# A state-space stage whose convolution of x moves from channels on partitions to tokens on partitions

## The chip, the cores and the metric

The kernel runs on one core of one Trainium2 chip. The core has TensorE (PE, matrix products into PSUM), VectorE (DVE, elementwise), ScalarE (ACT, functions and copies), GpSimd (POOL, elementwise on SBUF) and SyncE (SP, which only issues transfers), each with its own queue of instructions in the order in which the program wrote them, and 16 DMA engines that all queues share. The metric is the device time of one execution in microseconds, the median of several runs.

## The reference

The model is a decoder trunk of two layers on 256 tokens with 2048 features: a latent attention, a dense squared-ReLU MLP, a Mamba-2 state-space mixer and a second MLP, each behind an RMS norm and added to a residual stream. All of it is float32. The change is in the state-space mixer:

```python
def ssm_mixer(h, w_in, conv_w, conv_b, dt_bias, a_log, d_skip, norm_g, w_out):
    zxbcdt = h @ w_in                       # 256 x 2048 by 2048 x 10304
    z, xbc, dt = jnp.split(zxbcdt, [4096, 4096 + 6144], axis=-1)
    xbc = silu(causal_depthwise_conv(xbc, conv_w, conv_b))   # 4 taps over tokens, per channel
    xs, b_in, c_in = jnp.split(xbc, [4096, 4096 + 1024], axis=-1)
    dt = softplus(dt + dt_bias)
    a = -exp(a_log)
    y = ssd_chunked_scan(xs, dt, a, b_in, c_in)   # 8 groups of 8 heads of 64 features
    y = y + d_skip * xs
    y = y * silu(z)
    y = y * rsqrt(mean(y * y, per group) + eps) * norm_g
    return y @ w_out
```

The convolution gives each channel at token s the sum of its own four weights times that channel at tokens s-3 to s, plus a bias. The scan is one chunk of 256 tokens: per head a 256 x 256 matrix of decays times scores, applied to x times dt.

## The kernel before

Every weight matrix is streamed from HBM in units of 128 x 1024 float32 (512 KB): SP issues the load into one of six `raw` buffers (line 88), ACT copies it to a rounded half `wh` (line 103), DVE subtracts to get the remainder `wl` (line 104), and TensorE forms three products per tile, high by high, high by low and low by high (`products`, lines 362 to 364). `Flow.next` keeps loads up to six units and conversions three units ahead of TensorE; there are four `wh` and four `wl` buffers, so ACT's copy for a unit waits until TensorE has left the unit four before it. A unit in the state-space stage is twelve products of 512 columns.

`ssm_body` holds the stage. Its token list is `SSM_ORDER` (line 1441): blocks of eight units for B, C, x and z (512 output columns each, both halves of the tokens t = 0, 1 in two PSUM banks of 128 tokens x 512 channels), the narrow block for dt, and pieces of the output product (`o`, four units for each of four column blocks) as soon as two groups are gated. TensorE's order is written out by this list; what the other engines do, and TensorE's small products, is put between units by a small planner: `when(us, fn)` puts a function into a list with a due time, `small` does the same and keeps small TensorE work 2.6 apart, and `move(2.72)` after each unit advances the planner's clock and calls what has come due. A function called there writes its instructions at that place of every engine's queue.

One x block is one group of eight heads. After its last unit `x_done` evacuates the two banks (`evac`, line 1117), and `conv` works in two halves of 256 channels: four 128 x 128 transposes bring channels onto partitions (line 1128), ACT starts the sum with bias and fourth weight (line 1135), DVE adds the three shifted terms, a shift being an offset in the free dimension (line 1138, three per 128 channels), ACT takes the Silu (line 1139). Then `back(t)` transposes four times per half of the tokens (line 1257), copies out (line 1260), multiplies by dt on DVE (line 1262) and by the decay to the chunk's edge and by d on POOL (lines 1266, 1271), and queues the group in `waiting`. `heads(g)`, one group at a time, loads four decay rows spread to 128 partitions (`cm`, SP, line 1298), forms exponents and decays on ACT (lines 1305, 1309), multiplies by the scores `cb` on DVE (line 1313), and `product` applies them to x on TensorE (line 1322). `gate` multiplies by Silu of z, normalizes, and transposes for the output product (`turn`, line 1368). B and C go through the same `conv`.

The only waits that bind the queues to each other here are those on buffers: `scratch` tiles (eight), `xtm` (six) and `xd` (four) for x and x times dt, four `cm`, four PSUM banks for small work and four for accumulation.

Of the kernel before, what the change touches and what calls it, by code (L numbers as in the profile page):

```python
# [20 lines left out]
F32 = mybir.dt.float32  # L21
F32R = mybir.dt.float32r
I32 = mybir.dt.int32
AF = mybir.ActivationFunctionType
ALU = mybir.AluOpType
# [3 lines left out]
P = 128  # L29
# [7 lines left out]
GROUPS = 8  # L37
# [177 lines left out]
class Banks:  # L215
    name = "bank"
# [14 lines left out]
class Trunk:  # L231
# [849 lines left out]
    def ssm_body(self, sp, dp, gain):  # L1081
        nc, d, cst = self.nc, self.d, self.cst
        lhs_x = self.from_tiles(self.xT)
        xT, rs = self.xT, self.rs
# [13 lines left out]
        def small(us, fn, gap=2.6):  # L1098
            at[1] = max(at[0] + us, at[1] + gap)
            when(at[1] - at[0], fn)  # L1100
# [10 lines left out]
        diagonal = lambda: cst[:, C_TRI:C_TRI + P]  # L1111

        def evac(accs):
            ev = []
            for t in range(2):
                e = self.scratch()
                nc.scalar.activation(e, accs[t], AF.Copy, scale=rs[t])
                ev.append(e)
            return ev
# [38 lines left out]
        def cb_group(g):  # L1158
# [5 lines left out]
            t = sp.tile([P, 2, P], F32, name=f"cb{g}")  # L1164
            far[g] = sp.tile([P, 2, P], F32R, name=f"cf{g}")
# [77 lines left out]

        def x_done(g, accs):
            fmx = [None, None]
            ev = evac(accs)
            xg[g], xd[g] = [None, None], [None, None]

            def dst(j, a):
                fmx[j] = a  # L1250
                return a

            def back(t):
                b = self.ps(self.sm, "sm")
                for k in range(4):
                    o = (k % 2) * 256 + t * P
                    nc.tensor.transpose(b[:, k * P:(k + 1) * P], fmx[k // 2][:, o:o + P], self.ident)
                at[0] += 0.45
                x = sp.tile([P, 512], F32, tag="xtm", name=f"xtm{g}_{t}", bufs=XTM)
                nc.scalar.activation(x, b, AF.Copy)  # L1260
                w = sp.tile([P, 512], F32, tag="xd", name=f"xd{g}_{t}", bufs=XD)
                nc.vector.tensor_tensor(heads_of(w), heads_of(x), spread(dt[:, t], g), ALU.mult)
                xg[g][t], xd[g][t] = x, w
                if t == 0:
                    xw = self.scratch()
                    nc.gpsimd.tensor_tensor(heads_of(xw), heads_of(x), spread(edge[:, 0], g), ALU.mult)
                    xh = sp.tile([P, 512], F32R, tag="xh", name=f"xh{g}", bufs=1)
                    xl = self.s2.tile([P, 512], F32R, tag="s2", name=self.name("s2"))
                    self.split_out(xh, xl, xw)
                    small(8, lambda: across(xh, xl))  # L1270
                nc.gpsimd.tensor_tensor(heads_of(x), heads_of(x), spread(cst[:, C_DSK:C_DSK + 64], g), ALU.mult)
                if t:
                    waiting.append(g)
                    if len(waiting) == 1:
                        heads(g)
# [11 lines left out]
            def after():  # L1287
                small(10, lambda: back(0))
                small(10, lambda: back(1))

            conv(ev, 4 * g, dst, after)

        def heads(g):
# [43 lines left out]
            begin = 24 if g == 1 else 0  # L1337
# [12 lines left out]
        def gate(g):  # L1350
# [21 lines left out]
            lag = 14 if g == 1 else 10  # L1372
# [3 lines left out]

        done = {"B": lambda i, a: bc_done("B", i, a), "C": lambda i, a: bc_done("C", i, a), "x": x_done, "z": z_done}
# [44 lines left out]
XTM, XD = 6, 4  # L1422


def ssm_plan():
    out = []
    for step in SSM_ORDER:
# [7 lines left out]
        else:  # L1435
# [5 lines left out]
SSM_ORDER = ["B0", "dt0", "C0", "x0", "x1", "B1", "C1", "z0", "z1", "x2", "x3", "o0", "z2", "z3", "x4", "x5", "o1",  # L1441
             "z4", "z5", "x6", "x7", "o201", "z6", "z7", "o223"]
# [198 lines left out]
```

## Time and profile before

| what | value |
|---|---|
| median of three runs | 2307.21 us (2306.47 to 2308.12) |
| the profiled execution's own time | 2306.98 us |
| its span | 2305.2 us |
| TensorE busy | 2294.9 us |
| DVE busy | 1854.1 us |
| ACT busy | 1432.4 us |
| POOL busy | 182.7 us |
| granted TensorE clock | 1.00 throughout |

The profile is of one execution. Its page gives busy time per engine, the span in 40 slices, the DMA queues, the chain of work that ended last, the costliest groups of instructions by line, and the DMA issues with the median time from issue to landing. A group's row reads: line, engine, operation, what it writes and reads, count, total busy us, mean ns; then the engine's idle time before these instructions and what ended it. Products of TensorE overlap, so their single durations do not add up; distances between starts do. The state-space stage lies at about 969 to 1560 us.

### The profile page before, as it was taken

Reading aid. Unit: us, or ns where it says so; the run is one execution under the profiler, and the core shown is the slowest. Engines: PE = TensorE matmul, PEld = TensorE weight load, DVE = VectorE, ACT = ScalarE, POOL = GpSimd, SP = SyncE. Lnnn points to the kernel's source line nnn. Section 1 sums busy time; section 2 is a strip of 40 time slices with the busy share of each in tenths; the row PEclk is TensorE's granted clock in tenths of the full one; section 3 lists DMA queues with packets and bytes.
Section 4 is the critical chain, followed back from the end, with each engine's and each line's share of the span. In section 5 each row is a group of like instructions: output and inputs, shape, how many; then the busy total and the mean of one; then the engine's idle time right before and its main releaser. Section 6 shows DMA issues by size and latency. Waiting matters only on the chain.

```text
span 2305.2 us, 30566 instructions
## 1 busy us (share of the span) xinstructions
PE 2294.9 (100%) x11065; PEld 1905.9 (83%) x11065; DVE 1854.1 (80%) x2180; ACT 1432.4 (62%) x1986; POOL 182.7 (8%) x223
## 2 busy tenths in 40 slices
PE   9999999999999999999999999999999999999999
PEld 7888888888888888888888888888888888888887
DVE  7776697999899897677677676766989889889895
ACT  7775465566666656576656566565666656666663
POOL 1430000000000000001010111110000000000000
PEclk9999999999999999999999999999999999999999
DMA  8444687887887877655566656566687788787874
GB/s 320 146 132 151 205 233 240 265 240 247 265 244 248 267 215 241 197 184 182 187 198 193 207 177 214 187 193 201 203 260 231 251 266 249 239 270 240 250 229 161
DMA packets 146102, 508.68 MB, mean 221 GB/s; under 512 B 16480, under 2 KB 17184, under 8 KB 145952
## 3 DMA queue, kind: packets, MB, share of 16 engines
q1 hardware_dynamic: 137664, 477.30, 62.8%
q0 software_dynamic: 8064, 29.36, 7.7%
q8 instruction: 87, 1.43, 0.2%
q14 instruction: 63, 0.52, 0.1%
q10 hardware_dynamic: 224, 0.07, 0.0%
HBM read 504.51 MB, written 2.16 MB: 220 GB/s over the span
## 4 chain that ended last, share of the span: by engine, by line
PE 97%; issue 1%; DVE 1%; DMA 0%; ACT 0%; POOL 0%; SPq 0%; DVEq 0%; ACTq 0%; POOLq 0%
PE yp L363 9%; PE yp L364 9%; PE yp L362 9%; PE acc L362 8%; PE acc L364 8%; PE acc L363 8%; PE st L363 8%; PE st L364 8%; PE st L362 8%; PE acc L345 3%; PE acc L341 3%; PE acc L342 3%; PE sm L326 2%; PE a L341 1%; PE kv L341 1%
## 5 line engine op out<-in xcount | busy, mean ns | idle before, releaser
L104 DVE TENSOR_TENSOR wl<-wraw,wh 128x1024 fp32r<-128x1024 f32 (+2 forms) x818 | 991.6, 1226 | 307.3 <-ACT wh L103 298.0
L103 ACT ACTIVATE wh<-wraw 128x1024 fp32r<-128x1024 f32 (+2 forms) x818 | 858.0, 1053 | 574.8 <-PE yp L364 178.2
L363 PE MATMUL yp<-wl,k 128*128 128x512 f32 x896 | 348.9, 389 | 1.0 <-DVE wl L104 1.0
L362 PE MATMUL yp<-wh,k 128*128 128x512 f32 x896 | 349.8, 390 | 0.0
L364 PE MATMUL yp<-wh,k 128*128 128x512 f32 x896 | 348.8, 389 | 0.0
L362 PE MATMUL acc<-wh,xt 128*128 128x512 f32 x704 | 279.3, 397 | 0.0
L363 PE MATMUL acc<-wl,xt 128*128 128x512 f32 x704 | 274.4, 390 | 0.4 <-DVE wl L104 0.4
L364 PE MATMUL acc<-wh,xt 128*128 128x512 f32 x704 | 274.7, 390 | 0.0
L103 ACT ACTIVATE wh<-wrx 128x1024 fp32r<-128x1024 f32 x168 | 177.9, 1059 | 136.4 <-PE yp L364 109.5
L104 DVE TENSOR_TENSOR wl<-wrx,wh 128x1024 fp32r<-128x1024 f32 x168 | 204.0, 1220 | 36.6 <-ACT wh L103 36.3
L363 PEld LDWEIGHTS yp<-wl,k 128*128 128x128 f32 x896 | 168.3, 188 | 36.3 <-DVE wl L104 1.9
L364 PEld LDWEIGHTS yp<-wh,k 128*128 128x128 f32 x896 | 168.2, 188 | 35.0
L362 PEld LDWEIGHTS yp<-wh,k 128*128 128x128 f32 x896 | 168.3, 188 | 34.6
L362 PE MATMUL st<-wh,xt 128*128 128x512 f32 x448 | 176.8, 395 | 0.0
L363 PE MATMUL st<-wl,xt 128*128 128x512 f32 x448 | 174.8, 390 | 0.0
L364 PE MATMUL st<-wh,xt 128*128 128x512 f32 x448 | 174.8, 390 | 0.0
L364 PEld LDWEIGHTS acc<-wh,xt 128*128 128x128 f32 x704 | 132.1, 188 | 28.1
L363 PEld LDWEIGHTS acc<-wl,xt 128*128 128x128 f32 x704 | 132.4, 188 | 27.1 <-DVE wl L104 1.2
L362 PEld LDWEIGHTS acc<-wh,xt 128*128 128x128 f32 x704 | 132.3, 188 | 26.1 <-issue 0.2
L199 POOL DMA_DIRECT2D wrx<-mi x56 | 49.0, 876 | 1140.8 <-DVE wl L104 988.6
L362 PE MATMUL st<-wh,sN 128*128 128x512 f32 x336 | 132.3, 394 | 0.0
L364 PE MATMUL st<-wh,sN 128*128 128x512 f32 x336 | 130.9, 390 | 0.0
(318 smaller groups left out, 3558.4 us busy)
## 6 DMA issues: line engine op xcount, KB each, us to landing
wraw<-mi SPq DMA_DIRECT2D x256, 512.0 KB, 5.2
wraw<-mo SPq DMA_DIRECT2D x256, 512.0 KB, 5.2
wraw<-si SPq DMA_DIRECT2D x160, 512.0 KB, 4.4
wraw<-so SPq DMA_DIRECT2D x64, 512.0 KB, 4.1
wrx<-mi SPq DMA_DIRECT2D x56, 512.0 KB, 5.0
wrx<-mi POOLq DMA_DIRECT2D x56, 512.0 KB, 8.0
wraw<-wo SPq DMA_DIRECT2D x32, 512.0 KB, 3.9
wraw<-ukv SPq DMA_DIRECT2D x16, 512.0 KB, 4.5
```

Source lines behind the costliest of these rows:

```text
L103: self.last = nc.scalar.activation(h[:, v], raw[:, v], AF.Copy)
L104: nc.vector.tensor_tensor(lo[:, v], raw[:, v], h[:, v].bitcast(F32), ALU.subtract)
L199: nc.gpsimd.dma_start(st["b11"].tile, quarter(d, 1, 0), accum_op=ALU.add)
L326: self.nc.tensor.transpose(b[:, j * P:(j + 1) * P], src[:, j * P:(j + 1) * P], self.ident)
L341: nc.tensor.matmul(accs[t][:, :n], ah, wh[:, q, :], start=first and kt + q == 0, stop=False)
L342: nc.tensor.matmul(accs[t][:, :n], al, wh[:, q, :], start=False, stop=False)
L345: nc.tensor.matmul(accs[t][:, :n], lhs(kt + q, t)[0], wl[:, q, :], start=False, stop=en and q == nk - 1)
L362: nc.tensor.matmul(b, ah, wh, start=first and q == 0, stop=False)
L363: nc.tensor.matmul(b, ah, wl, start=False, stop=False)
L364: nc.tensor.matmul(b, al, wh, start=False, stop=last and q == 1)
```

## The change

x stays with tokens on partitions. After an x block ACT evacuates both banks, scaled, into one tile `ev` of 128 tokens x 2 halves of the channels x 2 halves of the tokens x 256 channels. For each half of the channels, `shifted` makes three shifted copies in `ex`: for a shift by m tokens the ACT queue issues a transfer inside SBUF of 128 - m rows of 2 KB to m partitions further down, and the GpSimd queue one of m rows of 1 KB that carries the last m tokens of the first token half to the first partitions of the second. The planner places `weighted` seven of its microseconds later, in four steps 2.2 apart on DVE: the three copies times their weights in one operation (1536 elements per partition), the unshifted one times its weight and plus the bias, two additions, the last addition, and then ACT's Silu straight into `xtm`. The weights and bias of 256 channels come spread to all partitions, from a new input `cx`, by SP, as one transfer of 640 KB per half into a single buffer, asked for after the second step of the half before. `finish` does what `back` did behind its copy. Groups go through this one at a time (`line`). x and z blocks alternate, B1 and C1 come later, the output pieces are dealt out differently, the scores have six buffers instead of eight, and group 1's later start (`begin`, `lag`) goes. B and C keep `conv`.

```diff
@@ -1109,6 +1109,9 @@
         heads_of = lambda v: v.rearrange("p (h f) -> p h f", h=8)
         spread = lambda v, g: v[:, 8 * g:8 * g + 8].unsqueeze(2).to_broadcast([P, 8, 64])
         diagonal = lambda: cst[:, C_TRI:C_TRI + P]
+        ex, ev, tap = sp.tile([P, 3, 2, 256], F32, name="ex"), sp.tile([P, 2, 2, 256], F32, name="ev"), {}
+        line = []
+        nc.gpsimd.memset(ex[0:3, :, 0], 0.0)
 
         def evac(accs):
             ev = []
@@ -1161,8 +1164,8 @@
             nc.tensor.matmul(b[:, 0:256], B[:, 0:P], C, start=True, stop=True)
             nc.tensor.matmul(b[:, 256:384], B[:, P:256], C[:, P:256], start=True, stop=True)
             at[0] += 0.65
-            t = sp.tile([P, 2, P], F32, name=f"cb{g}")
-            far[g] = sp.tile([P, 2, P], F32R, name=f"cf{g}")
+            t = sp.tile([P, 2, P], F32, tag="cb", name=f"cb{g}", bufs=6)
+            far[g] = sp.tile([P, 2, P], F32R, tag="cf", name=f"cf{g}", bufs=6)
             for i in range(2):
                 nc.vector.tensor_tensor(t[:, i], b[:, 2 * i * P:2 * i * P + P], diagonal(), ALU.mult)
             self.split_out(far[g][:, 0], far[g][:, 1], b[:, P:256])
@@ -1241,38 +1244,79 @@
 
             small(15, cums)
 
+        def taps(k):
+            if k < 2 * GROUPS:
+                w = sp.tile([P, 5, 256], F32, tag="cx", name=f"cx{k}", bufs=1)
+                nc.sync.dma_start(w.rearrange("p a n -> p (a n)"), d["cx"][k:k + 1].to_broadcast([P, 5 * 256]))
+                tap[k] = w
+
         def x_done(g, accs):
-            fmx = [None, None]
-            ev = evac(accs)
+            line.append((g, accs))
+            if len(line) == 1:
+                x_begin(g, accs)
+
+        def x_begin(g, accs):
             xg[g], xd[g] = [None, None], [None, None]
-
-            def dst(j, a):
-                fmx[j] = a
-                return a
-
-            def back(t):
-                b = self.ps(self.sm, "sm")
-                for k in range(4):
-                    o = (k % 2) * 256 + t * P
-                    nc.tensor.transpose(b[:, k * P:(k + 1) * P], fmx[k // 2][:, o:o + P], self.ident)
-                at[0] += 0.45
-                x = sp.tile([P, 512], F32, tag="xtm", name=f"xtm{g}_{t}", bufs=XTM)
-                nc.scalar.activation(x, b, AF.Copy)
-                w = sp.tile([P, 512], F32, tag="xd", name=f"xd{g}_{t}", bufs=XD)
-                nc.vector.tensor_tensor(heads_of(w), heads_of(x), spread(dt[:, t], g), ALU.mult)
-                xg[g][t], xd[g][t] = x, w
-                if t == 0:
-                    xw = self.scratch()
-                    nc.gpsimd.tensor_tensor(heads_of(xw), heads_of(x), spread(edge[:, 0], g), ALU.mult)
-                    xh = sp.tile([P, 512], F32R, tag="xh", name=f"xh{g}", bufs=1)
-                    xl = self.s2.tile([P, 512], F32R, tag="s2", name=self.name("s2"))
-                    self.split_out(xh, xl, xw)
-                    small(8, lambda: across(xh, xl))
-                nc.gpsimd.tensor_tensor(heads_of(x), heads_of(x), spread(cst[:, C_DSK:C_DSK + 64], g), ALU.mult)
-                if t:
-                    waiting.append(g)
-                    if len(waiting) == 1:
-                        heads(g)
+            for t in range(2):
+                nc.scalar.activation(ev[:, :, t], accs[t].rearrange("p (j n) -> p j n", j=2), AF.Copy, scale=rs[t])
+
+            def shifted(j):
+                v = ev[:, j]
+                for m in range(1, 4):
+                    nc.scalar.dma_start(ex[m:, m - 1], v[:P - m])
+                    nc.gpsimd.dma_start(ex[:m, m - 1, 1], v[P - m:, 0])
+                when(LAG[0], lambda: weighted(j))
+
+            def weighted(j):
+                tt = nc.vector.tensor_tensor
+                v, w = ev[:, j], tap[2 * g + j]
+                both = lambda i: w[:, i].unsqueeze(1).to_broadcast([P, 2, 256])
+
+                def one():
+                    tt(ex, ex, w[:, 1:4].unsqueeze(2).to_broadcast([P, 3, 2, 256]), ALU.mult)
+
+                def two():
+                    tt(v, v, both(0), ALU.mult)
+                    tt(v, v, both(4), ALU.add)
+
+                def three():
+                    taps(2 * g + j + 1)
+                    tt(ex[:, 0], ex[:, 0], ex[:, 1], ALU.add)
+                    tt(v, v, ex[:, 2], ALU.add)
+
+                def four():
+                    tt(v, v, ex[:, 0], ALU.add)
+                    for t in range(2):
+                        if j == 0:
+                            xg[g][t] = sp.tile([P, 512], F32, tag="xtm", name=f"xtm{g}_{t}", bufs=XTM)
+                        nc.scalar.activation(xg[g][t][:, j * 256:(j + 1) * 256], v[:, t], AF.Silu)
+                    if j == 0:
+                        when(LAG[1], lambda: shifted(1))
+                    else:
+                        when(LAG[2], finish)
+                        line.pop(0)
+                        if line:
+                            x_begin(*line[0])
+
+                for i, fn in enumerate((one, two, three, four)):
+                    when(LAG[4] * i, fn)
+
+            def finish():
+                x = xg[g]
+                for t in range(2):
+                    w = sp.tile([P, 512], F32, tag="xd", name=f"xd{g}_{t}", bufs=XD)
+                    nc.vector.tensor_tensor(heads_of(w), heads_of(x[t]), spread(dt[:, t], g), ALU.mult)
+                    xd[g][t] = w
+                    if t == 0:
+                        xw = self.scratch()
+                        nc.gpsimd.tensor_tensor(heads_of(xw), heads_of(x[0]), spread(edge[:, 0], g), ALU.mult)
+                        xh, xl = (self.s2.tile([P, 512], F32R, tag="s2", name=self.name("s2")) for _ in range(2))
+                        self.split_out(xh, xl, xw)
+                        small(LAG[3], lambda: across(xh, xl))
+                    nc.gpsimd.tensor_tensor(heads_of(x[t]), heads_of(x[t]), spread(cst[:, C_DSK:C_DSK + 64], g), ALU.mult)
+                waiting.append(g)
+                if len(waiting) == 1:
+                    heads(g)
 
             def across(xh, xl):
                 b = self.ps(self.sm, "sm")
@@ -1284,11 +1328,7 @@
                 nc.vector.tensor_tensor(heads_of(w), heads_of(b), spread(edge[:, 1], g), ALU.mult)
                 nc.gpsimd.tensor_tensor(xg[g][1], xg[g][1], w, ALU.add)
 
-            def after():
-                small(10, lambda: back(0))
-                small(10, lambda: back(1))
-
-            conv(ev, 4 * g, dst, after)
+            shifted(0)
 
         def heads(g):
 
@@ -1334,7 +1374,7 @@
 
                 when(2, done)
 
-            begin = 24 if g == 1 else 0
+            begin = 0
             for i in range(4):
                 when(begin + 3 + 2.2 * i, lambda i=i: exponent(i))
             when(begin + 11, decay)
@@ -1369,11 +1409,12 @@
                 at[0] += 0.45
                 self.split_out(yT[g][0][:, :, sl], yT[g][1][:, :, sl], b.rearrange("p (k n) -> p k n", k=4))
 
-            lag = 14 if g == 1 else 10
+            lag = 10
             small(lag, lambda: turn(0))
             small(lag, lambda: turn(1))
             small(lag + 2, lambda: gated.add(g))
 
+        taps(0)
         done = {"B": lambda i, a: bc_done("B", i, a), "C": lambda i, a: bc_done("C", i, a), "x": x_done, "z": z_done}
         accs = None
         for tok in ssm_plan():
@@ -1420,6 +1461,7 @@
 
 
 XTM, XD = 6, 4
+LAG = (7,0,4,14,2.2)
 
 
 def ssm_plan():
@@ -1438,8 +1480,7 @@
 
 
 X_AT = (1, 2, 3, 3)
-SSM_ORDER = ["B0", "dt0", "C0", "x0", "x1", "B1", "C1", "z0", "z1", "x2", "x3", "o0", "z2", "z3", "x4", "x5", "o1",
-             "z4", "z5", "x6", "x7", "o201", "z6", "z7", "o223"]
+SSM_ORDER = ["B0", "dt0", "C0", "x0", "z0", "x1", "z1", "B1", "x2", "C1", "o001", "x3", "o023", "z2", "x4", "z3", "x5", "o101", "z4", "x6", "z5", "x7", "o123", "z6", "o201", "z7", "o223"]
 
 
 B12 = "raw"
@@ -1615,6 +1656,8 @@
         a[f"mo{i}"] = pieces(f(mlp_w_out)[i])
     a["si"] = pieces(wi[:, :10240])
     a["sidt"] = narrow(wi[:, 10240:])
+    cx = np.concatenate([f(ssm_conv_w)[0][::-1, :4096], f(ssm_conv_b)[0][None, :4096]]).astype(np.float32)
+    a["cx"] = np.ascontiguousarray(cx.reshape(5, 16, 256).transpose(1, 0, 2)).reshape(16, 5 * 256)
     a["so"] = pieces(f(ssm_w_out)[0])
     a["g"] = np.stack([rows(f(mlp_norm_g)[0], 512), rows(f(mix_norm_g)[1], 512), rows(f(mlp_norm_g)[1], 512)])
     a["qg"] = rows(f(mla_q_norm_g)[0], 512)[0]
```

## The prediction

> **What bounds the kernel now.** I read the page's busy times and its chain first, then the busy times of the state-space stage alone (the window from the first work on block B0 to the last gated group), then TensorE's waits inside it.
>
> ```profile
> span 2305.2 us, 30566 instructions
> PE 2294.9 (100%) x11065; PEld 1905.9 (83%) x11065; DVE 1854.1 (80%) x2180; ACT 1432.4 (62%) x1986; POOL 182.7 (8%) x223
> ...
> PE 97%; issue 1%; DVE 1%; DMA 0%; ACT 0%; POOL 0%; SPq 0%; DVEq 0%; ACTq 0%; POOLq 0%
> ...
> 969.00:1560.00 591.00, 590.62 (x3169) 489.47 (x3168) 407.02 (x516) 370.83 (x568) 69.82 (x62) 1.00 0.61 192
> ...
> PE acc L363 <- DVE wl L104: 0.4, 1, 0.4
> ```
>
> The chain is TensorE for 97% of its length. In the stage (columns: PE, PEld, DVE, ACT, POOL busy us, granted clock 1.00, DMA share, GB/s) TensorE is busy 590.62 of 591 us, and its one wait for data there is 0.4 us. So a re-ordering of blocks can win almost nothing in this stage; only fewer TensorE instructions can, and any new wait of TensorE is paid in full. The profiled execution took 2306.98 us (span 2305.2 and 1.8 around it), 0.23 below the median 2307.21; my sum starts from 2306.98 and adds 0.2 at the end.
>
> **What goes from TensorE.** x is no longer transposed to channels and back.
>
> ```profile
> L1128 PE MATMUL sm<-cst,s x96: 270/272/273, 979.9 to 1495.2; 128*128 128x128 f32 x96
> ...
> L1257 PE MATMUL sm<-cst,s x64: 270/272/330, 1044.8 to 1511.9; 128*128 128x128 f32 x64
> ...
> 1336.88 0.39 PE L364 MATMUL acc<-wh,xt 128*128 128x512 f32 x1
> 1337.12 0.60 PE L1257 MATMUL sm<-cst,s 128*128 128x128 f32 x4
> 1337.47 0.48 PE L362 MATMUL acc<-wh,xt 128*128 128x512 f32 x1
> 1337.79 0.39 PE L363 MATMUL acc<-wl,xt 128*128 128x512 f32 x1
> 1338.02 0.40 PE L364 MATMUL acc<-wh,xt 128*128 128x512 f32 x1
> ```
>
> All 64 of line 1257 go, and of the 96 of line 1128 the 64 that belong to x (B and C keep their 32): 128 transposes in 32 batches of four. The 272 ns overlap, so the price is read from starts. Without a batch, starts follow each other by 0.23 us (1337.79 to 1338.02). From 1336.88 to 1337.79 are two steps, 0.46, and took 0.91: a batch costs 0.45 us. 32 x 0.45 = **14.4 us** less. That is all the change can gain, beside the 0.4 us wait.
>
> **What ACT and DVE get.**
>
> ```profile
> L104 DVE TENSOR_TENSOR wl<-wraw,wh 128x1024 fp32r<-128x1024 f32 x196 | 246.6, 1266 | 162.2 <-ACT wh L103 161.5
> ...
> L1135 ACT ACTIVATE s<-sm,cst 128x256 f32<-128x256 f32 x48 | 26.0, 551 | 1.4 <-DVE s L1138 1.4
> L1138 DVE SCALAR_TENSOR_TENSOR s<-sm,cst,s 128x255 f32<-128x255 f32 x48 | 22.5, 477 | 0.8 <-ACT s L1135 0.6
> ...
> L1313 DVE TENSOR_TENSOR cm<-cm,cb 128x512 f32<-128x512 f32 x32 | 20.7, 684 | 2.5 <-ACT cm L1309 2.5
> ...
> L1117 ACT ACTIVATE s<-acc,rs 128x512 f32<-128x512 f32 x24 | 15.7, 683 | 5.3 <-PE acc L364 5.3
> ...
> L1139 ACT ACTIVATE s<-s 128x512 f32<-128x512 f32 x16 | 10.0, 625 | 0.6 <-DVE s L1138 0.3
> L1260 ACT ACTIVATE xtm<-sm 128x512 f32<-128x512 f32 x16 | 9.4, 589 | 6.2 <-PE sm L1257 6.2
> ...
> L1226 ACTq DMA_DIRECT2D cumD<-s x1: 504/504/504, 1004.6 to 1004.6; - x1
> ...
> L199 POOL DMA_DIRECT2D wrx<-mi x56: 865/875/1082, 309.4 to 2225.6; - x56
> ```
>
> DVE loses 12 of the 477 ns per group, 45.8 us in eight groups. Per half it gains one operation of 1536 elements and five of 512. 512 take 684 ns and 1024 some 1.22 us undisturbed, so 1536 take 1.75; a half is 1.75 + 5 x 0.68 = 5.2 us, sixteen are 83. Net +37: 407 + 37 = 444 us of some 577, 77%. DVE does not become the bound by its sum. The unit with the 1.75 needs 2.97 of 2.72 us, 0.25 over; its slack below hides that. ACT loses four of 551, two of 589 and two of 625 ns per group (4.6 us), and gets four Silus of 256 columns (551 each by line 1135, 2.2) and six DMA issues of 504 ns (3.0): +0.6 per group, 5 us in all, hidden in the 37% of the stage in which ACT is idle (370.83 of 591 busy). POOL gets 48 issues of 875 ns, 42 us, beside its 70 busy ones.
>
> SP gets sixteen loads of weights, 640 KB each, which wait for DVE's second step. The weight loads behind them come back some 4 us after issue and run six buffers ahead of their conversion, so I take nothing; without that cover each costs its own landing, some 5 us, on TensorE. The earlier start of group 1's heads, the six buffers for the scores and the new order issue nothing that TensorE waits for; at most the 0.4 us wait goes.
>
> **What is new on the path: the wait for the shifts.** DVE's first step reads all three shifted copies. It stands in DVE's queue ahead of the next subtractions of weights, and TensorE waits for those. So the question is when three transfers of 127, 126 and 125 rows of 2 KB land.
>
> ```profile
> cm<-cumD SPq DMA_DIRECT2D x32, 256.0 KB, 6.0
> ...
> out<-x SPq DMA_DIRECT2D x2, 128.0 KB, 1.9
> ...
> cumD<-s ACTq DMA_DIRECT2D x1, 64.0 KB, 4.6
> cst<-cst ACTq DMA_DIRECT2D x1, 8.0 KB, 2.7
> ...
> q1 hardware_dynamic: 137664, 477.30, 62.8%
> ...
> q10 hardware_dynamic: 224, 0.07, 0.0%
> ...
> 0.00:57.63 57.63, 54.65 (x250) 45.11 (x251) 43.09 (x83) 40.48 (x73) 8.18 (x22) 1.00 0.87 320
> ```
>
> The trace has no transfer like these. The lower end is the cm load: 128 rows of 2 KB, four in a row, 6.0 us. The upper end is one DMA engine carrying all 127 rows of one transfer. ACT's queue shows how rows are dealt out: its two transfers have 128 and 64 rows, 192 packets; the other 32 of its 224 are 16 closing packets each. So all 16 engines worked with equal shares, 8 rows and 4 rows. 127 is prime: equal shares exist only for one engine. 126 rows give 14 engines 9 each, 125 give 5 engines 25 each. If those shares start at the same engine, it carries 127 + 9 + 25 = 161 rows, 330 KB. I take this end: equal shares are what the rows show, and no row shows unequal ones.
>
> [...]
>
> A busy engine moves, in the first 57.63 us (320 GB/s at a DMA share of 0.87), 320 / 16 / 0.87 = 23.0 GB/s, and over the whole run 477.30 MB in 62.8% of 16 x 2305.2 us, 20.6. I take 23.0, since it is busiest there and idles least inside a packet: 330 KB need 14.3 us. Around it some 2 us are fixed (1.9 and 2.7 us for the small transfers above). Weight loads go on beside it until DVE stands still and the buffers are full, some three, each 32.8 KB on this engine: 4.3 us.
>
> ```profile
> 1289.18 1.06 ACT L103 ACTIVATE wh<-wraw 128x1024 fp32r<-128x1024 f32 x1 [1.66 <-PE acc L364]
> ...
> 1291.90 1.06 ACT L103 ACTIVATE wh<-wraw 128x1024 fp32r<-128x1024 f32 x1 [1.66 <-PE acc L364]
> ...
> 1290.27 1.23 DVE L104 TENSOR_TENSOR wl<-wraw,wh 128x1024 fp32r<-128x1024 f32 x1 [1.49 <-ACT wh L103]
> ```
>
> A unit of TensorE is 2.72 us; ACT's copy for it takes 1.06, DVE's subtraction (lo) 1.23, three units ahead. Now one group by hand, from time 0, where TensorE leaves the last unit of the x block (unit 0); lo up to unit 3 is done or under way.
> - ACT evacuates to 1.4 and issues to 1.9, 2.4, 2.9. Its copies for units 4 and 5 end at 4.0 and 5.0, lo at 5.2 and 6.4. By the planner (7 us, next unit boundary) the first step stands here, at 6.4.
> - Landing: 1.9 + 2.0 + 14.3 + 4.3 = 22.5. First step to 24.3, lo 6 to 25.5. TensorE wanted unit 6 at 5 x 2.72 = 13.6: **11.9 us late**.
> - Then two adds, lo, two adds, lo, last add: 31.4. ACT's Silus wait for it and run to 32.5, three issues to 34.0; only then comes its copy for unit 9, lo 9 at 36.3. TensorE wanted it at 33.6: 2.7 late.
> - Second half: lo 11 at 38.7, first issue over at 33.0, landing 53.6, lo 12 at 56.6; wanted at 44.5: 12.1 late. Behind the next Silus unit 15 is 1.1 late.
>
> 27.8 us per group, eight groups 222. **2306.98 - 14.4 + 222 + 0.2 = 2514.8.** The bounds: if the three transfers start at different engines, 127 rows (260 KB, 11.3 us) with two loads beside them (2.9) land at 18.1; 19.7 GB/s (the stage: 192 / 16 / 0.61) and three loads land at 25.6. 16 halves by -4.4 or +3.1 us are -70 or +50, and the alignment of DVE's other work may add some 10 either way: own range 2435 to 2575.
>
> **The rivals.** *Even spread.* The three transfers land like the cm loads, 6 us after issue, at 8: the first step to 9.8, lo 6 to 11.0, 2.6 us before TensorE wants it. Nothing is paid, 2306.98 - 14.4 = 2292.6 (2290 to 2300). For it: the cm row is nearest in bytes. Against it: every row dealt out there is an equal share.
>
> *Spread, but late.* From lo 6 back (13.6 - 1.2 - 1.75) the shifts may land at 10.6, 8.7 us after the first issue; each further us costs 16 over all halves, so 0.9 us eats the gain. The GpSimd pieces could do that:
>
> ```profile
> wrx<-mi POOLq DMA_DIRECT2D x56, 512.0 KB, 8.0
> ```
>
> Evacuation 1.4, three issues 2.6 and these 8.0 make 12.0, 1.4 past the point: +22, time 2315. Against it: that row moves and adds 512 KB, the pieces have up to three rows of 1 KB, and the small transfers above take 1.9 to 2.7. With some 0.9 us it ends at no change.
>
> *DVE held up by POOL* at the end of a group is there before as well (the same products of x), so it has no price of its own.
>
> **How the numbers follow.** One engine 0.77: equal shares alone are shown, but by three row counts that all divide. Even spread 0.16. Spread but late 0.07: 0.03 no change, 0.04 slower. A measurement of this kernel can tell about 0.2%, 4.6 us. So faster 0.16, same 0.03, slower 0.81. Predicted 2514.8. The range that holds 8 in 10 must take in both ends, 2290 to 2575; the likeliest case's own is 2435 to 2575.
>
> **What would show it.** Right: the issue rows of the shifts on ACT's queue land in some 15 to 25 us, DVE's first step waits for them some 15 us, sixteen times, and TensorE waits for lo some 12 us after each; 32 fewer batches of transposes; DVE +37 us busy. Wrong: shifts that land within 8.7 us of the first issue, and no wait of TensorE in the stage; then the time is 2292.6. If they land late and TensorE waits far less, the slack of lo was larger than my hand run has it.

## The result and the profile after

The changed kernel takes **2541.11 us** (median of 4 runs, 2539.77 to 2541.84), the kernel before 2307.66 beside it (2306.47 to 2308.6): 1.1011 times as long, 95% interval 1.0992 to 1.103. Predicted were 2514.8. Below, a time with a range or an interval beside it is the median of four runs; every other variant was run once, and repeats of one variant lie up to 10 us apart.

First the page of the changed kernel: span, busy times, granted clock in 40 slices, ACT's queue, the chain, and the row of DVE's first step.

```profile
span 2538.0 us, 30487 instructions
PE 2329.5 (92%) x10937; PEld 1921.2 (76%) x10937; DVE 1881.7 (74%) x2180; ACT 1426.6 (56%) x1968; POOL 223.4 (9%) x272
...
PEclk9999999999999999888898888798999999999999
...
q10 hardware_dynamic: 6592, 12.46, 1.5%
...
PE 79%; DMA 12%; DVE 3%; ACTq 2%; ACT 2%; issue 1%; SPq 0%; DVEq 0%
...
L1276 DVE TENSOR_TENSOR ex<-ex,cx 128x1536 f32<-128x1536 f32 x16 | 28.1, 1759 | 219.1 <-DMA ex<-ev 219.1
```

The span is 232.8 us longer. TensorE's busy time grew by 34.6 us (2294.9 to 2329.5) although 128 transposes are gone; its idle time grew from 10.3 to 208.5, by 198.2. The chain now runs for 12% of its length through the shifts' transfers and for 2% through ACT's sequencer, and the clock is below full speed in the slices of the state-space stage alone.

Most of the stage as one window (columns: window, length, busy us of PE, PEld, DVE, ACT, POOL, granted clock, DMA share, GB/s):

```profile
969.00:1600.00 631.00, 480.17 (x2347) 388.24 (x2345) 333.28 (x408) 284.95 (x437) 81.49 (x83) 0.86 0.53 166
```

TensorE works 76% of it, where it worked all of the time before, and DVE 53% (333.28 of 631): no engine became the bound by its sum. TensorE's waits in the stage (columns: us in all, times, longest):

```profile
PE acc L363 <- DVE wl L104: 187.6, 20, 14.6
...
PE acc L362 <- ACT wh L103: 12.1, 6, 4.1
```

By the page DVE stands 219.1 us for the shifts, 13.7 in the mean of sixteen, and TensorE stands behind it for the subtractions of weights. One such half, from the timeline (start, length, work; in brackets the idle time before it and what ended it):

```profile
1319.36 1.06 ACT L103 ACTIVATE wh<-wraw 128x1024 fp32r<-128x1024 f32 x1 [7.05 <-issue]
...
1332.18 1.76 DVE L1276 TENSOR_TENSOR ex<-ex,cx 128x1536 f32<-128x1536 f32 x1 [10.51 <-DMA ex<-ev]
...
1335.13 0.80 PE L363 MATMUL acc<-wl,k 128*128 128x512 f32 x1 [8.12 <-DVE wl L104]
```

ACT's first issue of this half began at 1311.39: 20.8 us to DVE's first step.

In the chain by time this half and the next one are these pieces (start, length, what):

```profile
1312.05 6.39 ACTq L1266
...
1318.48 13.58 DMA ex<-ev
...
1341.60 21.83 DMA ex<-ev
```

Two places are lost in the first half, then: 6.39 us in which ACT is still busy issuing, and the transfers.

### The profile page after: what moved, and what is told of

It is laid out like the page before. It is cut to its first block, busy times and chain, and to the rows that moved or that the text cites. A ratio compares the mean times of both kernels' runs of the same rounds, so it can differ in the third digit from the quotient of the medians.

```text
span 2538.0 us, 30487 instructions
## 1 busy us (share of the span) xinstructions
PE 2329.5 (92%) x10937; PEld 1921.2 (76%) x10937; DVE 1881.7 (74%) x2180; ACT 1426.6 (56%) x1968; POOL 223.4 (9%) x272
## 3 DMA queue, kind: packets, MB, share of 16 engines
q10 hardware_dynamic: 6592, 12.46, 1.5%
## 4 chain that ended last, share of the span: by engine, by line
PE 79%; DMA 12%; DVE 3%; ACTq 2%; ACT 2%; issue 1%; SPq 0%; DVEq 0%
DMA ex<-ev 11%; PE yp L363 9%; PE yp L364 9%; PE yp L362 9%; PE st L363 7%; PE st L364 7%; PE st L362 7%; PE acc L363 5%; PE acc L364 5%; PE acc L362 5%; PE acc L341 3%; PE acc L345 3%; PE acc L342 3%; ACTq L1266 2%; DVE wl L104 2%; PE sm L326 1%
## 5 line engine op out<-in xcount | busy, mean ns | idle before, releaser
L363 PE MATMUL acc<-wl,xt 128*128 128x512 f32 x704 | 288.3, 409 | 146.1 <-DVE wl L104 146.1
L362 PE MATMUL acc<-wh,xt 128*128 128x512 f32 x704 | 288.4, 410 | 9.1 <-ACT wh L103 8.9
L364 PE MATMUL acc<-wh,xt 128*128 128x512 f32 x704 | 285.3, 405 | 0.0
L363 PEld LDWEIGHTS acc<-wl,xt 128*128 128x128 f32 x704 | 139.3, 198 | 180.6 <-DVE wl L104 152.3
L362 PEld LDWEIGHTS yp<-wh,k 128*128 128x128 f32 x896 | 168.2, 188 | 34.6
L1276 DVE TENSOR_TENSOR ex<-ex,cx 128x1536 f32<-128x1536 f32 x16 | 28.1, 1759 | 219.1 <-DMA ex<-ev 219.1
L362 PEld LDWEIGHTS acc<-wh,xt 128*128 128x128 f32 x704 | 138.6, 197 | 40.9 <-ACT wh L103 11.6
L364 PEld LDWEIGHTS acc<-wh,xt 128*128 128x128 f32 x704 | 139.4, 198 | 29.8
L362 PE MATMUL st<-wh,sN 128*128 128x512 f32 x336 | 132.4, 394 | 0.0
```

The source lines that it names most:

```text
L362: nc.tensor.matmul(b, ah, wh, start=first and q == 0, stop=False)
L363: nc.tensor.matmul(b, ah, wl, start=False, stop=False)
L364: nc.tensor.matmul(b, al, wh, start=False, stop=last and q == 1)
L1276: tt(ex, ex, w[:, 1:4].unsqueeze(2).to_broadcast([P, 3, 2, 256]), ALU.mult)
```

## The experiments

### How the rows are dealt out: 112 rows and 113

The edit for 112 rows; the other kernel has 113 in both places of the last line.

```diff
-        nc.gpsimd.memset(ex[0:3, :, 0], 0.0)
+        nc.gpsimd.memset(ex, 0.0)
-                    nc.scalar.dma_start(ex[m:, m - 1], v[:P - m])
+                    nc.scalar.dma_start(ex[m:m + 112, m - 1], v[:112])
```

> The changed kernel with the three shifted copies cut to 112 rows each (the last 16 - m rows are left out of the computation). Theory, equal shares: 112 = 16 x 7, so all 16 engines carry 7 rows of each transfer, 43 KB per engine, and the copies land like the cm loads some 6 us after the issue; DVE's first step waits at most 2 us, TensorE not at all: 2293 us (2288 to 2302), granted clock 1.00. Rival, slow inside SBUF (a transfer that reads and writes SBUF is slow whatever its row count): 12% fewer bytes, so 2510 to 2541. Rival, the rest of the change (order, DVE's extra 37 us): 2541.

> The same with 113 rows in each of the three copies (the last 15 - m rows are left out). 113 is prime. Theory, equal shares: each transfer runs on one engine and, if it is the same one, that engine carries 339 rows, 694 KB, against 161 rows in the changed kernel: at 23 GB/s 30 us instead of 14.3, so each of 16 halves some 16 us later than the changed kernel's: about 2795 us (2700 to 2900), with fewer bytes than there. If the three transfers start at different engines: 113 rows, 10 us, about 2480. Rival, slow inside SBUF: as with 112 rows, 2510 to 2541. Rival, the rest of the change: 2541.

Measured: 2336.67 us with 112 rows, **2763.45** with 113. Of the kernel with 112 rows, ACT's queue and the shifts' issue row on the page, and two waits of the stage:

```profile
q10 hardware_dynamic: 6368, 11.09, 1.7%
...
ex<-ev ACTq DMA_DIRECT2D x48, 224.0 KB, 6.4
```

```profile
DVE ex L1276 <- DMA ex<-ev: 58.8, 16, 6.9
...
PE acc L363 <- DVE wl L104: 24.9, 10, 6.7
```

Of the kernel with 113 rows, the same queue on the page, the issue line (durations min/median/max in ns) and TensorE's waits:

```profile
q10 hardware_dynamic: 5696, 11.18, 1.1%
```

```profile
L1266 ACTq DMA_DIRECT2D ex<-ev x48: 594/5193/14251, 1029.3 to 1909.3; - x48
```

```profile
PE acc L363 <- DVE wl L104: 254.5, 38, 18.2
PE acc L362 <- ACT wh L103: 107.5, 21, 9.7
```

The forecast for 113 rows held (2763 in 2700 to 2900), the one for 112 did not (2337 for 2293). One row more per transfer costs 427 us, and 113 rows, fewer bytes than the change moves, cost 222 more than the change. Bytes can't do that; the number of engines can. ACT's queue counts it. In the trace of before its 224 packets are 128 rows of 64 bytes, 64 rows of 1024 and 32 packets of 4 bytes, 16 for each of two transfers; I read these as a closing packet from each engine that takes part. With 112 rows 6368 = 192 + 5376 rows + 800 closing ones; without the 32 of before that is 768 for 48 transfers, 16 engines each. With 113 rows 5696 = 192 + 5424 + 80: 48 for 48 transfers, **one engine each**. In the change 6592 = 192 + 6048 + 352, and its trace has 352 packets of 4 bytes: 320 for sixteen triples, 20 engines a triple, which is 1 + 14 + 5. It is also the same engine for all three: by the times of the packets, the rows of the shifts with 113 rows move one at a time for 442 us of the 461 in which any moves, and never more than two at once. In the change they move one at a time for 175 us of 267, 11 a half. "Even spread" and "spread but late" fall for the change. They fall as a level too: with 112 rows the transfers land in 6.4 us, as the row of the cm load said, and the time is 2337, not 2293. What that is, the next kernels ask.

### All rows, but evenly spread

```diff
-                    nc.scalar.dma_start(ex[m:, m - 1], v[:P - m])
+                    nc.scalar.dma_start(ex[m:m + 112, m - 1], v[:112])
+                    nc.scalar.dma_start(ex[m + 112:, m - 1], v[112:P - m])
```

> The whole computation, each shifted copy as two transfers on ACT's queue: 112 rows and the 16 - m rows behind them (15, 14, 13). Theory, equal shares: 7 rows on each of 16 engines and one row on each of 15, 14 or 13; six issues of some 0.6 to 0.75 us on ACT (1.4 + 4.5 = 5.9 after the block's end), landing at some 9 to 11, just at the 10.6 that is free: 2293 to 2305, faster than before. Rival, slow inside SBUF: 2541 or more, since ACT issues six instead of three. Rival, the rest of the change: 2541.

Measured: **2353.38** (2350.8 to 2354.7), 1.0198 times before (1.0181 to 1.0215). The page's queue, the line of the added issues, and TensorE's waits:

```profile
q10 hardware_dynamic: 7712, 12.47, 1.8%
```

```profile
L1267 ACTq DMA_DIRECT2D ex<-ev x48: 785/828/1504, 1028.8 to 1527.8; - x48
```

```profile
PE acc L363 <- DVE wl L104: 28.3, 21, 4.5
PE acc L362 <- ACT wh L103: 12.4, 4, 4.2
```

The same bytes land where they did, from 48 more issues, and 188 of the 233 us are gone. The closing packets agree again: 7712 = 192 + 6048 + 1472; less 32 that is 90 a triple, 48 for the three of 112 rows and 15 + 14 + 13 for the pieces of 15, 14 and 13 rows. So the uneven deal costs 188 us by this kernel and 204 by the one with 112 rows, which also leaves 11% of the rows and the 48 issues out.

### No shifts at all, and the weights on another queue

```diff
-                    nc.scalar.dma_start(ex[m:, m - 1], v[:P - m])
-                    nc.gpsimd.dma_start(ex[:m, m - 1, 1], v[P - m:, 0])
+                    pass
```

`ex` is filled with zeros once, as with 112 rows.

> The changed kernel without any of the transfers inside SBUF (the convolution keeps only its unshifted term; all work of the engines stays). Theory, equal shares, and the rival of slow transfers inside SBUF alike: 2293 us (2288 to 2300), no wait of TensorE in the stage. Rival, the rest of the change is what costs: 2541, or a part of the 233 us that stays.

Measured: 2313.87. The page, and TensorE's first waits in the stage:

```profile
span 2311.9 us, 30286 instructions
...
PE 2288.3 (99%) x10937; PEld 1896.9 (82%) x10937; DVE 1876.8 (81%) x2180; ACT 1430.6 (62%) x1970; POOL 207.3 (9%) x224
```

```profile
PE sm L1407 <- DVE s L1401: 10.7, 2, 5.6
PE acc L363 <- DVE wl L104: 5.3, 5, 3.8
```

Even with no shift to wait for, the new stage is not faster than the old one: 21 us above 2292.6. TensorE's busy time fell by 6.6 us instead of 14.4, and 13.3 more idle us came in (2311.9 - 2288.3 against 10.3). One suspect was SP's queue, in which the loads of `cx` wait for DVE ahead of weight loads. The second kernel puts them on GpSimd's queue:

```diff
-                nc.sync.dma_start(w.rearrange("p a n -> p (a n)"), d["cx"][k:k + 1].to_broadcast([P, 5 * 256]))
+                nc.gpsimd.dma_start(w.rearrange("p a n -> p (a n)"), d["cx"][k:k + 1].to_broadcast([P, 5 * 256]))
```

> The kernel without transfers inside SBUF (2313.9 us, 21 above the 2292.6 of the sum), with the loads of the convolution's weights on GpSimd's queue instead of SyncE's. Theory, a blocked queue: these loads wait for DVE's second step, and in SyncE's queue they hold back the loads of the weight matrices behind them and land late themselves; on GpSimd's queue the 21 us go: 2293 to 2298. Rival, order and DVE's larger work: 2310 to 2316 as before.

Measured: 2319.34, no less. The suspect falls as the place of the 21 us. The loads do land late, though: DVE waits 16.0 us for them in the first of these kernels and 24.6 in the second, and TensorE 5.3 and 7.7 for DVE's subtractions.

### The order alone

In the kernel before, only the new block order and the start of group 1:

```diff
-            begin = 24 if g == 1 else 0
+            begin = 0
-            lag = 14 if g == 1 else 10
+            lag = 10
-SSM_ORDER = ["B0", "dt0", "C0", "x0", "x1", "B1", "C1", "z0", "z1", "x2", "x3", "o0", "z2", "z3", "x4", "x5", "o1",
-             "z4", "z5", "x6", "x7", "o201", "z6", "z7", "o223"]
+SSM_ORDER = ["B0", "dt0", "C0", "x0", "z0", "x1", "z1", "B1", "x2", "C1", "o001", "x3", "o023", "z2", "x4", "z3", "x5", "o101", "z4", "x6", "z5", "x7", "o123", "z6", "o201", "z7", "o223"]
```

> The kernel before with nothing but the new order of blocks (and without the later start of group 1's heads that went with the old one); the convolution of x stays on channels with its transposes. If the new order is part of the 21 us that stay without any transfer: 2315 to 2330. If, as the prediction had it, the order costs nothing: 2307 (2303 to 2311).

Measured: **2320.03** (2317.48 to 2320.75), 1.0057 times before (1.0042 to 1.0072). Its page, and TensorE's longest waits:

```profile
span 2317.8 us, 30569 instructions
...
PE 2299.6 (99%) x11065; PEld 1908.0 (82%) x11065; DVE 1850.6 (80%) x2180; ACT 1449.4 (63%) x2000; POOL 195.7 (8%) x223
```

```profile
PE sm L1257 <- ACT s L1139: 6.5, 3, 3.0
PE sm L1368 <- DVE s L1362: 1.7, 1, 1.7
```

The order costs 14 us without any of the rest. TensorE idles 18.2 us instead of 10.3, and its unchanged work takes 4.7 longer. Both waits are of small products on ACT and DVE; as I read it, the new order asks for results sooner. It also changes what ACT does between them, below. It may be the larger part of the 21 us; but the two kernels differ in their convolution, so that 14 cannot simply be taken off 21, and what makes up the 21 is not settled.

### Later steps, with the pieces on other queues

If the 6 us landings are only just too late, a later first step and no extra issues on ACT should win them back. `mend` puts the pieces and the `cx` loads on GpSimd's queue, `even_new` the pieces on SP's; `even_old` is `even_new` in the order of before, with its `begin` and `lag`; `even_new` has a `lag` of 14 throughout. The edit of `mend` to what moved 112 rows and the rest on ACT's queue (beside the `cx` loads, shown above, which it also asks for after the second step):

```diff
-                    nc.scalar.dma_start(ex[m + 112:, m - 1], v[112:P - m])
+                    nc.gpsimd.dma_start(ex[m + 112:, m - 1], v[112:P - m])
-LAG = (7,0,4,14,2.2)
+LAG = (12,0,4,14,2.2)
```

> The whole computation with three mends: each shifted copy as 112 rows on ACT's queue and 16 - m rows on GpSimd's; DVE's first step 12 planner us behind the evacuation instead of 7; the convolution's weights loaded by GpSimd's queue right behind the second step. If equal shares, the place of the first step and the blocked queue are all of it: 2293 to 2300, faster than before. If DVE's extra work or the order holds it up: 2310 to 2320.

> The whole computation in the new order: 112 rows of each shifted copy on ACT's queue, the 16 - m rows behind them on SyncE's, the first step 12 planner us behind, and four more planner us for the transposes of the gated groups. If even shares and a later first step take away all waits for shifts, what the kernel without transfers kept is left, less its 11 us of waits for gated groups: 2303 to 2315. If the even transfers still land too late: 2330 to 2350, as with 112 rows.

> The same as the run in the new order (112 rows on ACT, the rest on SyncE, first step 12 behind), but with the order of blocks of the kernel before and its later start of group 1's heads. The old order had no wait of TensorE worth naming, and the new one alone cost 14 us: 2293 to 2302, faster than before, if the order is what stayed. If DVE's larger work in bursts of two x blocks one behind the other is what stayed: 2310 or more.

Measured: `mend` 2360.57 (1.0235 times before, 1.0218 to 1.0252), `even_new` **2340.18** (1.0137, 1.012 to 1.0154), `even_old` 2361.32 (1.0242, 1.0224 to 1.026). DVE's wait in `mend`, and TensorE's in `even_new`:

```profile
DVE ex L1277 <- DMA ex<-ev: 94.2, 16, 8.0
```

```profile
PE acc L363 <- DVE wl L104: 30.7, 19, 4.1
```

None comes back to before, and the old order makes this convolution slower, not faster. `even_new` is the best version with the whole computation, and it is 1.4% slower than the kernel before. The later due time did not shorten DVE's wait in `mend` (58.8 us with 112 rows and a due time of 7), though there the pieces had moved to another queue as well. The next pair goes back to the transfers of the change.

### Where the first step stands

With the transfers of the change, its due time at 22 instead of 7, and z2 ahead of the first output piece:

```diff
-LAG = (7,0,4,14,2.2)
+LAG = (22,0,4,14,2.2)
-SSM_ORDER = ["B0", "dt0", "C0", "x0", "z0", "x1", "z1", "B1", "x2", "C1", "o001", "x3", "o023", "z2", "x4", "z3", "x5", "o101", "z4", "x6", "z5", "x7", "o123", "z6", "o201", "z7", "o223"]
+SSM_ORDER = ["B0", "dt0", "C0", "x0", "z0", "x1", "z1", "B1", "x2", "C1", "x3", "z2", "o001", "x4", "o023", "z3", "x5", "z4", "o101", "x6", "z5", "x7", "o123", "z6", "o201", "z7", "o223"]
```

> The changed kernel with its uneven transfers (127, 126, 125 rows), but DVE's first step 22 planner us behind the shifts instead of 7; for the plan to hold, z2 stands before the first output pieces, z3 before x5 and z4 before the next ones. Theory, it is the wait in DVE's queue that costs, not the load of the one engine: the transfers still take 16 to 23 us, DVE does not wait for them, and what stays is what the kernel without transfers kept: 2314 to 2335, granted clock at 0.99 or more. Rival, the one engine delays the weight loads too (it carries about 0.5 of its time in shifts beside 0.6 in weights): ACT waits for weights and the time stays above 2400.

Measured: 2530.41. DVE's wait in the stage:

```profile
DVE ex L1276 <- DMA ex<-ev: 215.0, 16, 17.9
```

215.0 for 219.1: the step hardly moved. Counted in the trace, it stands two or three subtractions behind the evacuation or the last addition of the half before in the change, and two to five here. The order that is written out by hand binds TensorE alone (line 1608 of the changed kernel names only PE); DVE's instructions are put in order when the kernel is built, and a due time doesn't decide it. For DVE, then, it is not so that a function called by the planner writes its instructions at that place of the queue, as the section on the kernel before has it. So the next kernel binds the first step behind the last subtraction that has been written by then:

```diff
-            nc.vector.tensor_tensor(lo[:, v], raw[:, v], h[:, v].bitcast(F32), ALU.subtract)
+            self.low = nc.vector.tensor_tensor(lo[:, v], raw[:, v], h[:, v].bitcast(F32), ALU.subtract)
-                    tt(ex, ex, w[:, 1:4].unsqueeze(2).to_broadcast([P, 3, 2, 256]), ALU.mult)
+                    with self.tc.issue_after(self.flow.low.ins):
+                        tt(ex, ex, w[:, 1:4].unsqueeze(2).to_broadcast([P, 3, 2, 256]), ALU.mult)
```

> The run with the late first step, with that step now bound behind the subtraction written just before it, so that the build cannot put it forward: it stands some eleven subtractions behind the last addition of the half before, where it stood two behind in the changed kernel and in the first late run. The transfers are the uneven ones (127, 126, 125 rows). Theory, it is the wait in DVE's queue that costs: transfers of 16 to 23 us land before the step is reached, DVE waits for them less than 2 us each, TensorE's waits go, and what stays is what the kernel without transfers kept: 2310 to 2335. Rival, the load of the one engine costs by itself (it holds back its share of every weight load): ACT waits for weights, and the time stays above 2400.

Measured: 2499.67 (2495.73 to 2499.92), 1.0838 times before (1.082 to 1.0856). The groups of the first step and of the second one (busy, mean ns, then idle time before it and its releasers):

```profile
L1277 DVE TENSOR_TENSOR ex<-ex,cx 128x1536 f32<-128x1536 f32 x16 | 28.0, 1752 | 0.0
L1280 DVE TENSOR_TENSOR ev<-ev,cx 128x512 f32<-128x512 f32 x16 | 11.1, 692 | 168.4 <-DMA ex<-ev 117.1 <-DMA cm<-cumD 31.8 <-issue 19.4
```

The first step waits for nothing now: it stands seven to eleven subtractions down. But the second step was not bound, and the build put it ahead of the first in all sixteen halves. It overwrites `ev`, which the transfers still read, and took the wait over, ahead of the same subtractions: TensorE still waits 138.8 us for them. A kernel with both steps bound was not run, so it stays open how much of the 188 us a late enough DVE order could hide.

### Products put ahead of the waits

To ask whether the half clock follows from TensorE's idling, 40 more products, whose result nobody reads, go ahead of each half's wait.

```diff
+                    bank = self.ps(self.sm, "sm")
+                    h, v2 = lhs_x(0, 0)[0], xT[0][0][:, 0:2].rearrange("p a b -> p (a b)")
+                    for _ in range(40):
+                        nc.tensor.matmul(bank, h, v2, start=True, stop=True)
```

> The changed kernel with 40 extra products of 512 columns (9.1 us) on TensorE in each half, put just ahead of the unit at which it waits for DVE; their result is not used. Theory: of the 233 us, some 49 are no wait but products at half the granted clock (TensorE's busy time rose by 34.6 us although 14.4 us of transposes went), which follows 9 us of idle; the extra products lie in the wait, keep TensorE busy, and the clock stays near 1.00: 2541 - 49 = 2492 (2485 to 2515, a wait shorter than 9.1 us pays the difference). Rival: the clock falls for another reason, for example with the traffic inside SBUF; then it stays at 0.955 and the time is 2541 or more.

Measured: 2659.49. The page:

```profile
span 2657.6 us, 31748 instructions
...
PE 2460.6 (93%) x11577; PEld 2030.3 (76%) x11577; DVE 1888.7 (71%) x2180; ACT 1417.7 (53%) x1960; POOL 223.2 (8%) x272
```

TensorE idles 197.0 us, hardly less than the 208.5 of the change, and the products came on top (131 us more busy). They did not fill the waits, so this run does not answer the question; the trace of the change does, in the part on the clock below.

## Why the prediction was right, and where its steps were not

**The bound, and what a wait costs: right.** TensorE had 10.3 idle us to give away, and 198.2 were added to them one for one. The span's growth splits without rest: 198.2 idle, and 34.6 busy = -14.4 for the transposes + 49.

**The deal of the rows: right.** "Equal shares are what the rows show" is shown by the closing packets of four kernels and by 112 rows against 113. The counts all fit equal shares: 20 for 127, 126 and 125 rows together, which is 1 + 14 + 5, 16 for 112, one for 113, and 42 for 15, 14 and 13 together, one a row. That the shares start at the same engine, which the sum took, is shown for 113 rows, where 2763 were measured and different engines would have made it 2480 by the estimate on record.

**The landing: right in size.** From its first issue to DVE's step the hand run had 21.1 us (1.4 to 22.5); the half shown took 20.8. The next took 24.3, from the start of its first issue at 1339.25 to 1363.5. It is made up otherwise: in the half shown the three issues took 7.0 us of it, where the sum had 1.5, and what was left of the transfers 13.6. In the next half the rows of the tail, from 1352 to 1363, start one behind the other, some 12 a microsecond. The 13.7 us that DVE waits in the mean were "some 15".

**TensorE's lateness: right in size, not in its path.** 27.8 us a group were worked out; 187.6 + 12.1 over eight groups are 25.0. But part of it goes through ACT. The sum took 0.5 us for an issue; here they took up to 7.1:

```profile
L1266 ACTq DMA_DIRECT2D ex<-ev x48: 605/754/7121, 1027.5 to 1697.8; - x48
```

In the half shown ACT's copy of weights stood 7.05 us behind them. TensorE waited 3.13 us for that copy, before it waited 8.12 us for the subtraction behind DVE's step:

```profile
1320.47 0.80 PE L362 MATMUL acc<-wh,k 128*128 128x512 f32 x1 [3.13 <-ACT wh L103]
```

**The term that was missing: the clock.** Most of the 49 us are products at half speed. Around the half above (columns as in the windows before):

```profile
1327.00:1331.00 4.00, 0.01 (x1) 0.00 (x0) 0.00 (x0) 0.34 (x1) 0.00 (x0) 0.88 0.07 26
1331.00:1335.00 4.00, 0.00 (x0) 0.00 (x0) 2.82 (x3) 0.00 (x0) 0.00 (x0) 0.50 0.01 4
1335.00:1339.00 4.00, 3.87 (x9) 3.10 (x10) 4.00 (x7) 0.00 (x0) 0.00 (x0) 0.50 0.64 153
1339.00:1343.00 4.00, 4.00 (x16) 3.20 (x16) 4.00 (x6) 1.98 (x2) 1.51 (x3) 0.84 0.86 318
1343.00:1347.00 4.00, 4.00 (x20) 3.30 (x19) 4.00 (x6) 3.94 (x6) 0.00 (x0) 1.00 0.93 262
```

The clock falls some 3 us into the stall, and after it the first 4 us hold 9 products where a later 4 us hold 20. If it comes back once, 0.84 over four us puts that at 1340.3, 5.2 us after the first product; half of that, 2.6, is lost. The trace has 18 such stretches in the stage. TensorE is busy for 89.4 us of them and half of that, 44.7, is lost, 2.5 a stretch; some 4 of the 49 stay open. When it falls and returns is in the trace's clock records. Each of the 18 stretches is a whole number, one to six, of 3.413 us long, and so is each full one between them, one to 18. The windows of that length just ahead of a fall were busy for 0 to 49%, those just ahead of a return for 92 to 100%. Here one ran from 1336.88 to 1340.29, the first that products fill, and the clock came back at its end. Traffic inside SBUF is not needed for it: the kernel without shifts (granted clock 0.997) falls to half clock three times, each behind a wait of TensorE of 3.8 us or more.

The prediction had no such term: each of the 18 stretches should have been priced 2.5 us. The sum fell short by only 26, because its idle time of 222 was 24 too high. That it came so near is in part luck: the two errors have opposite signs.

**"The new order issues nothing that TensorE waits for": wrong.** Nothing was the price; alone in the kernel before, the order costs 14 us, and the waits that it makes are on ACT's Silu and DVE's last step of the gate.

**ACT: its sum missed the table loads.** The 5 us more of the prediction include 24 of issues, which the page doesn't count as busy; without them ACT's busy time should have fallen by 19 us, and it fell by 5.8. What the sum left out is loads of function tables in the stage. Before, and then after:

```profile
L1139 ACT ACT_TABLE_LOAD x5 | 6.4, 1283 | 0.7 <-DVE s L1138 0.6
L1309 ACT ACT_TABLE_LOAD x5 | 6.4, 1283 | 0.1
L1346 ACT ACT_TABLE_LOAD x4 | 5.1, 1283 | 0.1
```

```profile
L1349 ACT ACT_TABLE_LOAD x12 | 15.4, 1283 | 0.2
L1292 ACT ACT_TABLE_LOAD x9 | 11.5, 1283 | 0.2
L1142 ACT ACT_TABLE_LOAD x4 | 5.1, 1283 | 0.1
L1386 ACT ACT_TABLE_LOAD x3 | 3.8, 1283 | 0.1
```

14 became 28, 18 us of ACT. The kernel with the order alone has 28 too, so they belong to the order. That they are why its small products come late is argued, not shown.

**DVE and POOL: near.** DVE got 27.6 us more for the 37 worked out, POOL 40.7 for 42. Neither set the end.

**The 14.4 us of transposes** show as 6.6 in the kernel without shifts. By its trace TensorE is busy there for 12.0 us at half clock, which loses 6.0, and 6.6 and 6.0 are 12.6. So the term stands to within 2 us.

**"By the planner the first step stands here, at 6.4": right in place by luck.** The due time doesn't place it; the build's own order of DVE does, and it happened to be about there. A reader who had trusted the due time would have mended the change with it, in vain.

**SP's loads of `cx` at nothing: nearly.** Moving them off SP's queue won nothing. But without shifts DVE waits 16.0 us for them, behind which at most the 5.3 us of TensorE lie; in the change the shifts land later, and the page puts all of DVE's wait down to these.

**The rivals.** Even spread at 2292.6 would have been wrong for an even spread as well: 2337 to 2361. The middle one, "spread but late", describes those kernels: each landing is a little behind its point, TensorE waits 28 us in all with 112 rows and 41 with all of them on ACT's queue, and the time is 2337 to 2361 where it had 2315. It, too, had no half clock, which by the same working takes 14 us with 112 rows and 14 with all of them on ACT's queue (granted clock 0.993 in both).

## What to carry to other kernels

Before a transfer between partitions goes on a path, count its rows: 112 in 16 shares and a second issue for the rest cost 188 us less here than 127, 126 and 125 rows in one issue each. Price a stall of TensorE with the half clock behind it (2.5 us each here). Look at every instruction that touches the tile of a transfer, and not only at the one that waits: binding one step further down gave most of the wait to another step, which the build had put ahead of it. An order of blocks is a change of its own; time it alone.

## What the runs showed that was not expected

- TensorE did not stand still for a whole window of 3.413 us ahead of every fall of its clock. In the change it fell behind windows that were busy for up to 49%, and stayed full behind one of 46% and all above 49%.
- An issue on ACT's queue is not a fixed cost. It took 518 to 1909 ns where the 48 transfers were spread over 16 engines, 605 to 7121 with the rows of the change, and up to 14251 with one engine each. In the half shown ACT ran nothing else meanwhile.
- In the change's packets a row of 2 KB inside SBUF takes 84 ns in the median: 161 of them are 13.5 us, against the 14.3 that were worked out from the weight loads. With 112 rows, on 16 engines, it takes 108.
- GpSimd's small pieces of 1 and 3 rows of 1 KB took nearly as long to land as the 224 KB transfers of the kernel with 112 rows, 6.4 us:

```profile
ex<-ev POOLq DMA_DIRECT2D x16, 1.0 KB, 5.8
...
ex<-ev POOLq DMA_DIRECT2D x16, 3.0 KB, 5.2
```
